# Turning a norm's column into a row: four fp32 products with the identity in place of two ones-by-diagonal products

## The chip, the cores and the metric

The kernel runs on one core of one Trainium2 chip. The metric is the device time of one execution in microseconds (us); lower is better. A core has a matrix engine (PE, with its weight loads shown as PEld), a vector engine (DVE), an activation engine (ACT), a general engine (POOL) and a queue engine (SP) that issues most loads. Each engine runs its own instructions strictly in the order in which the program placed them; an instruction that waits holds all that stand behind it on that engine.

## The reference

One decoder layer on x of 512 tokens by 1024: a SwiGLU feed-forward (FFN 1, width 2816), a mixer (a state-space group "SSD" with 16 heads in 4 groups, and differential attention with 8 heads, sharing an input and an output projection), cross-attention into a memory of 256 tokens, a second feed-forward (FFN 2), a final norm. What matters here is the norm:

```python
def rms_norm(x, w):
    x32 = x.astype(jnp.float32)
    y = x32 * lax.rsqrt(jnp.mean(x32 * x32, axis=-1, keepdims=True) + EPS)
    return y.astype(x.dtype) * w
...
    yg = y.reshape(bsz, seqlen, SSD_GROUPS, SSD_WIDTH // SSD_GROUPS)
    yg = yg * lax.rsqrt(jnp.mean(yg * yg, axis=-1, keepdims=True) + EPS)
```

It is taken over x ahead of FFN 1, the mixer, the cross-attention and FFN 2, over the memory, and over each of the four SSD groups: one number per token each time. (The heads' norm and the final norm don't use the code below.)

## The kernel before

Activations lie transposed: features on the 128 partitions, tokens along the free dimension (512 fp32 numbers, which is one accumulator bank). So one number per token is needed as a *row*: the same 512 numbers on every partition. The square sums come out of the matrix engine as a *column* (`nps` or `pn`, 128 partitions x 4 blocks of tokens); `inv_rms_cols` makes `ncol`, 1/rms, on DVE (`nv`) and POOL (`pow`). In the SSD groups `rh` is half of it.

`row_of(col, nb, first, second)` turns the column into a row in the bank `nrow`. It splits the column into a high part `ch` (rounded to fp32r, the format in which the matrix engine takes one pass) and a rest `cl`, builds for each a diagonal `ndiag` (identity times column, 128 x 512), and multiplies a matrix of ones (`ones_r`, stationary) with the two diagonals, adding both in `nrow`. The engine of the diagonals is DVE for the five `Stat` norms (FFN 1, memory, mixer, cross, FFN 2) and POOL for the four SSD groups. `Stat.finish` then copies `nrow` to `row` on ACT; the SSD group multiplies `y` with `nrow` on DVE (L935), and splits the result into `ysh` (ACT) and `ysl` (DVE).

All large products are made in three fp32r products of high and low parts. `load_w` loads a weight tile (`wr`, 6 buffers), and splits it into `wh` on ACT and `wl` on DVE (3 buffers each). Products accumulate in 8 banks, 4 named acc and 4 aux. The names of accumulators tell the stage: `pv`, `pq`, `pk` the attention's projections, `pxbc`, `pz` the SSD group's, `pm` the output projections, `pcv` the values of the cross-attention, `pst`, `pf`, `py` the SSD scan, `pcb` four 128 x 128 products of two fp32 tensors at the start of each SSD group, `qa`, `qb`, `qe` the FFN quads.

The order of the work is fixed when the program is built. `Order` runs a dense stream of projections and side chains (the SSD groups, the heads, the norms). Its clock `od.t` is advanced by `mm` with each product (one pass for fp32r, four for fp32), and a chain's `yield W[...]` says how much of that clock is to pass before its next step is written. The engines' own order of ACT and DVE comes from a list scheduler on the same program; SP and POOL stand as written.

Around the third SSD group (g = 2) the dense stream is `pz`, then `out_attn(1, 5, 8)`: three output tiles `pm` of 12 products each, for x[5], x[6], x[7], then `pcv`. The raw weights of these three tiles are loads of `in_woa`; `memory_prep` loads eight tiles `mem` there.

Of the kernel before, what the change touches and what calls it, by code (L numbers as in the profile page):

```python
# [11 lines left out]
F32 = mybir.dt.float32  # L12
R32 = mybir.dt.float32r
AF = mybir.ActivationFunctionType
ALU = mybir.AluOpType
AX = mybir.AxisListType

P = 128
# [82 lines left out]
def body(tc, a, dbg=None):  # L101
# [6 lines left out]
    tiny = ctx.enter_context(tc.tile_pool(name="tiny", bufs=6))  # L108
# [6 lines left out]
    def nm(s):  # L115
        uid[0] += 1
        return f"{s}_{uid[0]}"

    def s2(s, dt=F32, shape=(P, T)):
        if math.prod(shape[1:]) <= T // 2:  # L120
            return sp.tile(list(shape), dt, tag="s1", name=nm(s), bufs=NHALF)
        return sp.tile(list(shape), dt, tag="s2", name=nm(s))
# [4 lines left out]
    def small(s, n, bufs=None):  # L127
        return tiny.tile([P, n], F32, tag=s, name=nm(s), bufs=bufs)
# [4 lines left out]
    def aux(s, shape=(P, T)):  # L133
        return aux_p.tile(list(shape), F32, tag="aux", name=nm(s))
# [5 lines left out]
    last, start, last_sum, recent, newest, newest_mm = [], [], [], [], [], []  # L140
    V, S, G = nc.vector, nc.scalar, nc.gpsimd
    od = Order()

    def mm(out, w, x, start, stop):
        od.t += (1 if w.dtype == R32 else 4) * (x.free_size() + 8) / 2400
        newest_mm[:] = [nc.tensor.matmul(out, w, x, start=start, stop=stop).ins]  # L146
# [36 lines left out]
    @contextmanager  # L183
    def behind(ins):
        with ExitStack() as after:
            for i in ins:
                after.enter_context(tc.issue_after(i))
            yield
# [146 lines left out]
    ident = cp.tile([P, P], F32, name="ident")  # L335
# [3 lines left out]
    ones_r = cp.tile([P, P], R32, name="ones_r")  # L339
# [13 lines left out]
    def inv_rms_cols(ps, nb, scale, eps):  # L353
        v = small("nv", nb)
        V.tensor_scalar(v, ps, scale, eps, ALU.mult, ALU.add)
        col = small("ncol", nb, bufs=6)
        G.tensor_tensor(col, v, mhalf[:, :nb], ALU.pow)
        return col

    def row_of(col, nb, first, second):  # L360
        ch = tiny.tile([P, nb], R32, tag="ch", name=nm("ch"))
        V.tensor_copy(ch, col)
        cl = small("cl", nb)
        V.tensor_tensor(cl, col, ch.bitcast(F32), ALU.subtract)
        pr = aux("nrow", (P, nb * P))
        for j, (eng, c) in enumerate(((first, ch.bitcast(F32)), (second, cl))):
            diag = s2("ndiag", R32, (P, nb, P))
            eng.tensor_tensor(diag, ident[:, None, :].to_broadcast([P, nb, P]), c[:, :, None].to_broadcast([P, nb, P]), ALU.mult)  # L368
            with behind(list(newest_mm)):
                mm(pr, ones_r, diag.rearrange("p a b -> p (a b)"), j == 0, j == 1)  # L370
        return pr

    class Stat:
# [14 lines left out]
        def finish(self, apart=2.5):  # L388
            nb = self.n // P
            ps = aux("nps", (P, nb))  # L390
            for b in range(nb):
                mm(ps[:, b : b + 1], self.acc[:, b * P : (b + 1) * P], ones[:, 0:1], True, True)
            self.col = inv_rms_cols(ps, nb, 1.0 / D, EPS)
            yield apart
            pr = row_of(self.col, nb, V, V)
            self.row = s2("row", shape=(P, nb * P))
            S.activation(self.row, pr, AF.Copy)

# [408 lines left out]
    def group_dense(g):  # L807
        bc, xs, zs = [], [], []
        yield from xbc_tile(8 + g, bc)
        yield from xbc_tile(12 + g, bc)  # L810
        for j in range(2):
            yield from xbc_tile(2 * g + j, xs)
        od.spawn(group(g, bc[0], bc[1], xs, zs), W["g0"])
        for j in range(2):
            ps = acc("pz")
            yield from proj(ps, load_w(a["wz"][2 * g + j]), h)
            zs.append(silu2(ps))
# [11 lines left out]
    def group(g, bt, ct, xs, zs):  # L829
# [99 lines left out]
        rh = small("rh", 4)  # L929
        V.tensor_scalar(rh, rr, 0.5, None, ALU.mult)  # L930
        yield W["gn"]
        pr = row_of(rh, 4, G, G)
        for j in range(2):
            n = 2 * g + j
            V.scalar_tensor_tensor(yz[j], yz[j], par[:, C_SSD + n : C_SSD + n + 1], pr, ALU.mult, ALU.mult)  # L935
# [468 lines left out]
```

## Time and profile before

| what | us |
|---|---|
| median of 3 runs (1333.7, 1337.35, 1333.83) | 1333.83 |
| the profiled execution | 1333.16 |
| its span, first to last instruction | 1331.4 |
| PE busy | 1305.6 (98%) |
| DVE busy | 976.2 (73%) |
| ACT busy | 663.0 (50%) |
| POOL busy | 112.3 (8%) |

The profiled execution is 0.67 us under the median; 1.8 us of it lie outside the span. A row of the profile's timeline reads: start in the span (us), duration (us), engine, line of the code, operation, output tile and input tiles, count, and in brackets how long the engine sat idle before it and what ended that. In a row of waits, `PE pm L146 <- ACT wh L155: 5.7, 1, 5.7` says that PE's instruction writing `pm` waited for ACT's `wh`: total us, times, longest. An fp32 product shows as two instructions, so four of them as x8; ends of products are modelled, so what one costs in a busy stream is read from start to start.

### The profile page before, as it was taken

The page shows a single profiled execution, that of the slowest core. Times are in us where ns is not written, and L with a number is a line of the kernel's source. Part 1 is how long each engine was busy: PE and PEld are TensorE (multiplying, and loading weights), DVE is VectorE, ACT ScalarE, POOL GpSimd, SP SyncE. Part 2 cuts the span into 40 slices and gives each one's busy share as a digit, 9 for nine tenths or more (in the row PEclk, how much of TensorE's full clock was granted, in tenths as well). Part 3 has the DMA queues.
Part 4 walks back from the last instruction along what each step waited for, and adds up shares of the span by engine and source line. Part 5 has one row for each costly group of instructions (what it writes and reads, how often), then busy time and mean ns, then how long its engine had stood idle before and what let it go on. Part 6 is the DMA issues. An engine that isn't in the chain of part 4 may idle for free. (4 is left out here: it accounts for less than half of the span.)

```text
span 1331.4 us, 20052 instructions
## 1 busy us (share of the span) xinstructions
PE 1305.6 (98%) x7769; PEld 1136.6 (85%) x7769; DVE 976.2 (73%) x1528; ACT 663.0 (50%) x1114; POOL 112.3 (8%) x127
## 2 busy tenths in 40 slices
PE   8999999999999999999999989999999999999997
PEld 7898998899887778777788868888889999989995
DVE  6874778487885786647767776656678878887896
ACT  6442445154453564336644645434455545554564
POOL 0000010000010011200112021120001100000001
PEclk9999999999999999999999999999999999999999
DMA  7444577556464435763276477786239776666762
GB/s 271 111 127 127 127 198 246 134 145 172 128 234 151 126 87 128 225 200 99 60 208 197 109 205 225 200 208 173 61 114 244 205 224 175 190 193 174 194 200 95
DMA packets 67999, 222.71 MB, mean 167 GB/s; under 512 B 8424, under 2 KB 11984, under 8 KB 67552
## 3 DMA queue, kind: packets, MB, share of 16 engines
q1 hardware_dynamic: 52400, 174.42, 39.3%
q0 software_dynamic: 11904, 40.45, 17.1%
q10 hardware_dynamic: 3600, 6.56, 1.5%
q8 instruction: 61, 1.00, 0.3%
q14 instruction: 34, 0.28, 0.1%
HBM read 219.24 MB, written 50.91 MB: 203 GB/s over the span
## 5 line engine op out<-in xcount | busy, mean ns | idle before, releaser
L155 ACT ACTIVATE wh<-wr 128x1024 fp32r<-128x1024 f32 (+2 forms) x311 | 316.8, 1021 | 382.7 <-PE po L146 61.7
L156 DVE TENSOR_TENSOR wl<-wr,wh 128x1024 fp32r<-128x1024 f32 (+2 forms) x311 | 367.2, 1183 | 116.9 <-ACT wh L155 114.0
L146 PE MATMUL po<-gh,wh 128*128 128x512 f32 x176 | 68.8, 392 | 0.0
L146 PE MATMUL po<-gl,wh 128*128 128x512 f32 x176 | 68.5, 390 | 0.0
L146 PE MATMUL po<-gh,wl 128*128 128x512 f32 x176 | 68.4, 389 | 0.0
L240 PE MATMUL qa<-hml,wh 128*128 128x256 f32 x216 | 61.1, 283 | 0.0
L240 PE MATMUL qa<-hmh,wl 128*128 128x256 f32 x216 | 61.1, 283 | 0.0
L240 PE MATMUL qa<-hmh,wh 128*128 128x256 f32 x216 | 61.1, 283 | 0.0
L146 PE MATMUL pxbc<-hnh,wh 128*128 128x512 f32 x128 | 52.1, 407 | 0.0
L146 PE MATMUL pxbc<-hnl,wh 128*128 128x512 f32 x128 | 50.2, 392 | 0.0
L146 PE MATMUL pxbc<-hnh,wl 128*128 128x512 f32 x128 | 50.2, 392 | 0.0
L706 ACT ACTIVATE ec<-ec,mn 128x512 f32<-128x512 f32 (+3 forms) x64 | 35.5, 555 | 24.8 <-DVE mn L705 24.7
L511 DVE TENSOR_TENSOR upd<-po,row 128x512 f32<-128x512 f32 x24 | 16.6, 690 | 39.1 <-PE po L146 38.8
L240 PE MATMUL qe<-s31h,wl 128*128 128x256 f32 x152 | 43.2, 284 | 0.5 <-DVE wl L156 0.5
L240 PE MATMUL qb<-s24h,wl 128*128 128x256 f32 x152 | 43.1, 284 | 0.5 <-DVE wl L156 0.5
L240 PE MATMUL qe<-s31h,wh 128*128 128x256 f32 x152 | 43.1, 284 | 0.0
L240 PE MATMUL qe<-s24h,wh 128*128 128x256 f32 x152 | 43.0, 283 | 0.0
L240 PE MATMUL qb<-hmh,wh 128*128 128x256 f32 x152 | 43.0, 283 | 0.0
L240 PE MATMUL qb<-hml,wh 128*128 128x256 f32 x152 | 43.0, 283 | 0.0
L240 PE MATMUL qb<-hmh,wl 128*128 128x256 f32 x152 | 43.0, 283 | 0.0
L240 PE MATMUL qe<-s24h,wl 128*128 128x256 f32 x152 | 43.0, 283 | 0.0
L240 PE MATMUL qb<-s31h,wl 128*128 128x256 f32 x152 | 43.0, 283 | 0.0
(444 smaller groups left out, 4063.3 us busy)
## 6 DMA issues: line engine op xcount, KB each, us to landing
wr<-in_f2q SPq DMA_DIRECT2D x44, 512.0 KB, 4.4
wr<-in_f1q SPq DMA_DIRECT2D x40, 512.0 KB, 4.1
isum<-in_f2q SPq DMA_DIRECT2D x22, 512.0 KB, 5.7
wr<-isum SPq DMA_DIRECT2D x22, 512.0 KB, 4.4
wsum<-in_f2b SPq DMA_DIRECT2D x20, 512.0 KB, 6.2
wr<-wsum SPq DMA_DIRECT2D x20, 512.0 KB, 4.2
wr<-in_f1q POOLq DMA_DIRECT2D x16, 512.0 KB, 5.6
wr<-in_f1o SPq DMA_DIRECT2D x16, 512.0 KB, 4.0
```

The lines of the kernel that those rows point to most:

```text
L146: newest_mm[:] = [nc.tensor.matmul(out, w, x, start=start, stop=stop).ins]
L155: S.activation(hi, src, AF.Copy),
L156: V.tensor_tensor(lo, src, hi.bitcast(F32), ALU.subtract),
L240: newest_mm[:] = [nc.tensor.matmul(out, a_[:, wc], b_, start=first and f == 0 and kp == 0 and j == 0, stop=kp == n - 1 and j == 2, skip_gr ...
L511: V.tensor_tensor(upd, po, row4, ALU.mult)
L706: S.activation(ec[:, :n], ec[:, :n], AF.Exp, bias=mn, scale=-1.0, accum_out=sm[c][:, i : i + 1])
```

## The change

`row_of` no longer splits the column and builds no diagonals. For each block of 128 tokens it takes one column of `col`, read with step zero as a 128 x 128 stationary operand (the same number in all columns), and multiplies it with the identity in plain fp32. The product is the column's numbers as a row on all partitions. Four products write the four quarters of `nrow` (two for the memory's norm).

```diff
-    def row_of(col, nb, first, second):
-        ch = tiny.tile([P, nb], R32, tag="ch", name=nm("ch"))
-        V.tensor_copy(ch, col)
-        cl = small("cl", nb)
-        V.tensor_tensor(cl, col, ch.bitcast(F32), ALU.subtract)
+    def row_of(col, nb):
         pr = aux("nrow", (P, nb * P))
-        for j, (eng, c) in enumerate(((first, ch.bitcast(F32)), (second, cl))):
-            diag = s2("ndiag", R32, (P, nb, P))
-            eng.tensor_tensor(diag, ident[:, None, :].to_broadcast([P, nb, P]), c[:, :, None].to_broadcast([P, nb, P]), ALU.mult)
-            with behind(list(newest_mm)):
-                mm(pr, ones_r, diag.rearrange("p a b -> p (a b)"), j == 0, j == 1)
+        with behind(list(newest_mm)):
+            for b in range(nb):
+                mm(pr[:, b * P : (b + 1) * P], col[:, b : b + 1].to_broadcast([P, P]), ident, True, True)
         return pr
...
-            pr = row_of(self.col, nb, V, V)
+            pr = row_of(self.col, nb)
...
-        pr = row_of(rh, 4, G, G)
+        pr = row_of(rh, 4)
```

Everything below `row_of` stands six lines higher in the changed file (L929 is the old L935). Up to the first SSD group the order of the matrix engine's instructions is the same but for `nrow`. After it, the clock `od.t` stands 0.47 us further on at each row (four passes of 4 x 136 columns in place of two of 520, at its 2400 columns per us), and some side steps move against the dense stream by three products or so. Three places of the third SSD group:

On ACT, ahead of that group, where the weights of the output tiles are split (`wh` of a 512-wide `wr`; `wh_7808` and `wh_7838` before are those of x[5] and x[6]). Before:

```order
L155 ACTIVATE wh_7808<-wr_7806 128x512
L920 ACTIVATE ysq_7676<-y_7669 128x512
L799 ACTIVATE conv_7685<-pxbc_7627,par 128x512
L155 ACTIVATE wh_7838<-wr_7836 128x512
L790 ACTIVATE th_1555_7690<-conv_7685 128x512
```

And now (`wh_7776` is that of x[5]):

```order
L155 ACTIVATE wh_7776<-wr_7774 128x512
L914 ACTIVATE ysq_7638<-y_7549 128x512
L914 ACTIVATE ysq_7641<-y_7634 128x512
L793 ACTIVATE conv_7653<-pxbc_7595,par 128x512
L784 ACTIVATE th_1535_7658<-conv_7653 128x512
```

The split for x[6] has left this place.

On ACT, some rows later: from the group's normed output `ysh` through the next group's decays (`e`, `gate`) to the next weights. Before (`wh_7922` is that of x[7]):

```order
L155 ACTIVATE ysh_7857<-y_7584 128x512
L155 ACTIVATE ysh_7862<-y_7669 128x512
L890 ACTIVATE e_1604_7872<-gate_7580 64x512 x2
L892 ACTIVATE gate_7580<-gate_7580,cum 128x128 x5
L893 ACTIVATE gate_7580<-gate_7580 128x512
L892 ACTIVATE gate_7580<-gate_7580,cum 128x128 x3
L159 ACTIVATE hm_7903<-mem_7887,par 128x256
L893 ACTIVATE gate_7580<-gate_7580 128x512
L159 ACTIVATE hm_7915<-mem_7889,par 128x256
L155 ACTIVATE wh_7922<-wr_7920 128x512
```

And now (`wh_7861` is that of x[6], `wh_7884` that of x[7]):

```order
L155 ACTIVATE ysh_7808<-y_7549 128x512
L155 ACTIVATE ysh_7813<-y_7634 128x512
L884 ACTIVATE e_1576_7823<-gate_7545 64x512 x2
L886 ACTIVATE gate_7545<-gate_7545,cum 128x128 x5
L887 ACTIVATE gate_7545<-gate_7545 128x512
L886 ACTIVATE gate_7545<-gate_7545,cum 128x128 x3
L159 ACTIVATE hm_7854<-mem_7838,par 128x256
L887 ACTIVATE gate_7545<-gate_7545 128x512
L155 ACTIVATE wh_7861<-wr_7859 128x512
L159 ACTIVATE hm_7874<-mem_7840,par 128x256
L155 ACTIVATE wh_7884<-wr_7882 128x512
```

Two weight splits now stand behind the decays where one stood, and one `hm` fewer is ahead of the first. On SP the load of x[6]'s weights likewise stands behind the eight `mem` loads now, and stood ahead of them.

On PE at the same place: the row, between the scan's `pst` and the output tiles (`pm_7835` and `pm_7858` are x[6]). Before:

```order
L146 MATMUL pst_7828<-xde_7765,btk_7797 128x256
L146 MATMUL pm_7835<-yah_6302,wh_7838 128x512
L146 MATMUL pm_7835<-yal_6303,wh_7838 128x512
L146 MATMUL pm_7835<-yah_6302,wl_7839 128x512
L146 MATMUL nrow_7849<-ndiag_7850,ones_r 128x512
L146 MATMUL nrow_7849<-ndiag_7853,ones_r 128x512
L146 MATMUL pst_7866<-xde_7788,btk_7797 128x256
L146 MATMUL pm_7835<-yah_6480,wh_7838 128x512
```

And now:

```order
L146 MATMUL pm_7773<-yah_6850,wl_7777 128x512
L146 MATMUL pst_7797<-xde_7744,btk_7765 128x256
L146 MATMUL nrow_7802<-ident,rh_7735 128x128 x4
L146 MATMUL pst_7817<-xde_7756,btk_7765 128x256
L146 MATMUL pm_7858<-yah_6267,wh_7861 128x512
```

The row stands three products earlier, and with it all of x[6]'s 12 products stand behind the row.

## The prediction

> **What bounds the kernel.** I read the page's busy times first, then PE's table of waits.
>
> ```profile
> PE 1305.6 (98%) x7769; PEld 1136.6 (85%) x7769; DVE 976.2 (73%) x1528; ACT 663.0 (50%) x1114; POOL 112.3 (8%) x127
> ```
>
> PE is busy 98% of the span, so a microsecond of PE work is a microsecond of the end, and work taken off DVE or POOL counts only where PE waits for it. Where does it wait?
>
> ```profile
> PE pm L146 <- ACT wh L155: 5.7, 1, 5.7
> ...
> PE pv L146 <- DVE kl L156: 2.2, 1, 2.2
> PE pt L150 <- DVE on L766: 1.3, 1, 1.3
> ```
>
> Three waits matter, each once. The first two lie beside a `nrow`, so the sum has three parts: PE's own work for the nine rows, the wait of `pv`, and the wait of `pm`.
>
> **PE's work for the rows.** Before, a row is two products; read from its start to the start of the next instruction.
>
> ```profile
> 367.13 1.10 PE L146 MATMUL nrow<-ndiag,ones_r 128*128 128x512 f32 x2 [0.33 <-DVE ndiag L368]
> 368.07 0.40 PE L146 MATMUL pck<-hm,wh 128*128 128x256 f32 x2
> ...
> 569.31 0.62 PE L146 MATMUL nrow<-ndiag,ones_r 128*128 128x512 f32 x2
> 569.77 0.40 PE L146 MATMUL pv<-wh,hnh 128*128 128x512 f32 x1
> ...
> 878.53 1.01 PE L146 MATMUL nrow<-ndiag,ones_r 128*128 128x512 f32 x2
> 879.37 0.39 PE L146 MATMUL pcq<-hmh,wh 128*128 128x512 f32 x1
> ...
> 1004.08 0.40 PE L146 MATMUL nrow<-ndiag,ones_r 128*128 128x512 f32 x1
> 1005.02 0.50 PE L146 MATMUL nrow<-ndiag,ones_r 128*128 128x512 f32 x1 [0.55 <-DVE ndiag L368]
> 1005.36 0.27 PE L240 MATMUL qb<-s31h,wh 128*128 128x256 f32 x1
> ```
>
> Undisturbed a row costs 0.46 (569.31 to 569.77). I take that for the four SSD groups and, as an estimate, for FFN 1's row. The memory's, half as wide, is taken as 0.23; the mixer's costs 0.33 + 0.94 = 1.27, the cross-attention's 0.84, FFN 2's 1.28: the last three wait for the second diagonal, which DVE makes more slowly than PE uses it. Sum: 5 x 0.46 + 0.23 + 1.27 + 0.84 + 1.28 = 5.9 us.
>
> After, a row is four fp32 products of 128 columns. The same thing stands in the trace: `pcb` is four of them, with four stationary tiles, into one bank.
>
> ```profile
> 516.31 1.05 PE L146 MATMUL pcb<-th,th 128*128 128x128 f32 x8
> 517.20 0.60 PE L150 MATMUL pxt<-ident,th 128*128 128x128 f32 x4
> 517.55 0.48 PE L146 MATMUL pz<-hnh,wh 128*128 128x512 f32 x1
> 517.87 0.40 PE L146 MATMUL pz<-hnl,wh 128*128 128x512 f32 x1
> ```
>
> It takes 0.89 us. The first wide product behind a run of short ones takes 0.32 (517.55 to 517.87), 0.09 over the 0.23 of its kind in the rows at 788 below. So 8 x 0.98 for the full rows and 0.45 + 0.09 for the memory's: 8.4 us. The column is ready before its old diagonals were, and the row's place in PE's stream isn't earlier than that, so I count no wait. **This part: +8.4 - 5.9 = +2.5 us.** That leaves open what a stationary operand read with step zero costs; nothing in the trace loads one. The low end is `pcb`'s own price, nothing added. The high end is that each of the 68 loads (34 products, two each) stands bare once more, at
>
> ```profile
> L146 PEld LDWEIGHTS pcb<-th,th x32: 187/192/192, 516.1 to 777.2; 128*128 128x128 f32 x32
> ```
>
> 68 x 0.192 = 13.1 us. I take the low end: `pcb` is the same load but for the step.
>
> **The removed DVE and POOL work.** DVE loses 18 small operations and ten diagonals. Its cover is PE's stream: apart from the waits counted above, no PE wait hangs on them, so they count for nothing. POOL loses its eight diagonals, and one pair of them is on the path, though nothing waits for it. DVE's timeline:
>
> ```profile
> 561.86 3.45 DVE L156 TENSOR_TENSOR wl<-wr,wh 128x1024 fp32r<-128x1024 f32 x1
> 565.23 0.68 DVE L156 TENSOR_TENSOR kl<-pk,kh 128x512 fp32r<-128x512 f32 x1
> ```
>
> POOL at that time:
>
> ```profile
> 561.89 1.32 POOL L368 TENSOR_TENSOR ndiag<-ident,ch 128x512 fp32r<-128x512 f32 x1
> 562.90 1.31 POOL L368 TENSOR_TENSOR ndiag<-ident,cl 128x512 fp32r<-128x512 f32 x1
> ```
>
> And all splits of that size, grouped (busy us, mean ns of one):
>
> ```profile
> L156 DVE TENSOR_TENSOR wl<-wr,wh 128x1024 fp32r<-128x1024 f32 x280 | 344.0, 1230 | 111.3 <-ACT wh L155 109.2 <-DMA isum<-in_f2q 0.5 <-DMA wr<-in_wcq 0.2
> ```
>
> And PE in that stretch:
>
> ```profile
> 563.39 0.39 PE L146 MATMUL pv<-wh,hnh 128*128 128x512 f32 x1
> 565.96 0.50 PE L146 MATMUL pv<-wh,hnh 128*128 128x512 f32 x1 [2.18 <-DVE kl L156]
> ```
>
> This `wl` takes 3.45 us where the mean of 280 is 1.23. The 2.2 us too many are the stretch from 561.9 to 564.2 in which POOL makes its diagonals: DVE's operation on two SBUF inputs stands still meanwhile. `kl` is queued behind it, and PE waits for `kl` because that frees the bank of the fourth `pv`. Without the diagonals `wl` ends near 563.0 and `kl` near 563.7, when PE needs it (563.62). Of the 2.57 us between the two `pv`, 0.23 is work; I also count the 0.1 by which PE's first product after a wait is longer. **This part: -2.4 us.** Ends: 0 if something else holds `kl`, -2.4.
>
> **The wait of `pm`, third SSD group.** PE's timeline:
>
> ```profile
> 788.43 0.39 PE L146 MATMUL pm<-yal,wh 128*128 128x512 f32 x1
> 788.66 0.39 PE L146 MATMUL pm<-yah,wl 128*128 128x512 f32 x1
> 794.71 0.79 PE L146 MATMUL pm<-yah,wh 128*128 128x512 f32 x1 [5.67 <-ACT wh L155]
> ```
>
> DVE just before:
>
> ```profile
> 786.10 0.42 DVE L871 TENSOR_TENSOR st<-st,cdec 128x256 f32<-128x256 f32 x1
> 786.59 1.41 DVE L935 SCALAR_TENSOR_TENSOR y<-y,par,nrow 128x512 f32<-128x512 f32 x2
> ```
>
> And ACT, the start and the end of its block:
>
> ```profile
> 787.37 1.29 ACT L155 ACTIVATE ysh<-y 128x512 fp32r<-128x512 f32 x2 [2.70 <-DVE y L935]
> ...
> 793.65 0.49 ACT L159 ACTIVATE hm<-mem,par 128x256 fp32r<-128x256 f32 x1
> 794.05 0.61 ACT L155 ACTIVATE wh<-wr 128x512 fp32r<-128x512 f32 x1
> ```
>
> PE has finished x[6] and waits for x[7]'s weights, which ACT splits only behind `ysh` and the decays, without a pause from 787.37 on. In the new order the weights of x[6] stand there too. So PE gets no further than the third `pst`, and waits with 24 products to do instead of 12: 12 x 0.227 = 2.7 us more work behind the wait. What does it get back? The row stands 0.9 us earlier on PE, but DVE's `y` has `st` at 786.10 to 786.52 ahead of it either way, so ACT's block starts only some 0.13 earlier; and one `hm` fewer (793.65 to 794.05, 0.40) precedes the split. **This part: +2.7 - 0.5 = +2.2 us**; the wait itself grows from 5.7 to about 8. Ends: 0 if the place of x[6]'s split doesn't matter, +2.7 if ACT starts no earlier.
>
> Behind the wait the clock matters. The busy time of the engines in one stretch, with the granted clock third from the end:
>
> ```profile
> 794.70:800.90 6.20, 6.19 (x15) 4.71 (x16) 4.97 (x9) 4.11 (x6) 0.00 (x0) 0.50 0.69 232
> ```
>
> For 6.2 us PE's granted clock is 0.50, which costs 3.1 us. By this row the longer wait costs the same, and the sum is unchanged. The Trainium skill (TensorE: Matmul & The Clock Gate, section "What's actually happening") has a free-running window of about 3.4 us: half speed after an idle window, full speed after a busy one. By that, an estimate, the slow stretch lasts 3.4 to 6.8 us and costs 1.7 to 3.4, so the sum would lie between 1.4 us lower and 0.3 higher, differing from one execution to the next. The trace agrees that a stall of 5.7 us is followed by half speed; how the stretch varies no run here shows.
>
> **Moved steps elsewhere.** Between 590 and 640 us the heads' steps slide by about three products against `pq` and `pk`, which changes PE's cover there. Some waits may shrink and others grow; a new one is priced by the 1.3 us of `pt`, either way. I take 0.
>
> **The sum.** +2.5 - 2.4 + 2.2 = +2.3 us on the profiled execution's 1333.16: 1335.5. The median of the runs lies 0.67 above that execution, which is the noise of a run; I keep 1335.5, that is 0.1% over the median. What a measurement here can tell from no change is 0.3%, 4.0 us: faster is under 1329.8, slower over 1337.8.
>
> **Rivals.**
> 1. *The long wait goes.* If x[6]'s and x[7]'s weights come before PE needs them, 5.7 + 3.1 us vanish: 1333.2 + 2.5 - 2.4 - 8.8 = 1324.5. For it: the row is ready earlier. Against it: ACT's order is fixed, and `ysh` and the decays, 6.7 us from 787.37 to 794.05, stand ahead of the split. Chance 0.05, and 0.03 for smaller gains beyond the bound.
> 2. *The step-zero load is slow.* It ends on the slower side: 1333.2 + 2.3 + up to 13.1 = 1348.6. It decides from 2.3 us, that is 0.034 us for each of the 68 loads. Against it: the load is of one number a partition instead of 128. Chance 0.08.
> 3. *New waits among the heads or behind the long one.* Two of 1.3 us on top of the sum: 1338.1. For it: the steps do move, and DMA and ACT run only some microseconds ahead. Chance 0.12, three quarters of it beyond the bound.
> 4. *The wait of `pm` stays as it was*: 1333.16 + 0.1 = 1333.3. Chance 0.14.
> 5. *The wait of `pv` stays*, because the loads that feed DVE are late and not POOL's diagonals: 1335.5 + 2.4 = 1337.9, about on the bound. Chance 0.08.
>
> My forecast, between 1333.5 and 1337.5, has the remaining 0.50.
>
> **Range and chances.** From 1331.0 (the forecast with the shortest slow stretch, or the case where `pm`'s wait doesn't grow and one wait of 1.3 us goes) to 1339.5 (two new waits and a slow median); left out are rival 1, rival 2 and a little of the third. Faster 0.08. Slower: 0.08 of rival 2, 0.09 of rival 3 and 0.02 of rival 5, 0.19. Same: 0.73.
>
> **What would show it.** Nine `nrow` groups of x8 (x4 for the memory) at 0.89 from start to next start, with no `ndiag` among PE's waits; a `wl` of 1.2 us near 562 and no wait of `pv` for `kl`; a wait of `pm` for `wh` of about 8 us near 786, with both x[6] and x[7] behind it and a granted clock of 0.5 after it. Rows well over 0.89 would be rival 2; a `pm` wait of 6 us or none would prove the third part wrong; new rows in PE's table of waits are rival 3.

## The result and the profile after

| kernel | median us | lowest to highest | runs | ratio to before, 95% |
|---|---|---|---|---|
| before, beside it | 1333.98 | 1332.95 to 1337.35 | 14 | |
| changed | 1331.93 | 1330.42 to 1333.81 | 14 | 0.9981 [0.9973, 0.9988] |

The change makes the kernel 0.19% faster, 2.5 us by the ratio, with an interval from 1.6 to 3.6. That is inside the 0.3% at which "same" ends, and inside the range of the prediction; but the forecast was +2.3 us, and the sign is the opposite. The profiled execution of the changed kernel took 1332.84 us, 0.9 over its median, where that of before lies 0.8 under its own (1333.16 beside 1333.98). So the two traces differ by 0.3 us only, and the accounts below go by places and not by the two spans.

The page's busy times after:

```profile
PE 1307.9 (98%) x7819; PEld 1141.0 (86%) x7819; DVE 966.2 (73%) x1500; ACT 663.3 (50%) x1114; POOL 103.3 (8%) x119
```

PE is busy 2.3 us longer, DVE 10.0 shorter, POOL 9.0 shorter. And the waits of PE, as in the table of before:

```profile
PE pm L146 <- ACT wh L155: 7.4, 1, 7.4
...
PE qb L240 <- ACT u L299: 1.4, 1, 1.4
PE qe L240 <- DVE nlam L556: 0.8, 1, 0.8
```

The wait of `pv` for `kl` (2.2) is gone, as forecast; the wait of `pm` has grown from 5.7 to 7.4. But the wait of `pt` for `on` among the heads (1.3) is gone too, which was not forecast, and a new one of `qb` for ACT's `u` stands in FFN 2. The wait of `qe` for `nlam`, 0.75 us at 202.94, is in this trace alone of the twelve kept; e4 and e5, which have the same program up to there, don't have it. So I take it for this execution's and not for the change's; it is as large as most of the 0.9 us above the median.

The rows themselves, on PE's timeline:

```profile
366.67 1.05 PE L146 MATMUL nrow<-ident,ncol 128*128 128x128 f32 x8
367.48 0.48 PE L146 MATMUL pck<-hm,wh 128*128 128x256 f32 x2
...
566.51 1.05 PE L146 MATMUL nrow<-ident,rh 128*128 128x128 f32 x8
567.32 0.48 PE L146 MATMUL pv<-wh,hnh 128*128 128x512 f32 x1
567.63 0.39 PE L146 MATMUL pv<-wl,hnh 128*128 128x512 f32 x1
...
1002.45 1.05 PE L146 MATMUL nrow<-ident,ncol 128*128 128x128 f32 x8
1003.25 0.36 PE L240 MATMUL qb<-s31h,wh 128*128 128x256 f32 x1
```

A row takes 0.81 us from its start to the next start (566.51 to 567.32), no row waits for its column, and the first product behind it takes 0.31 (567.32 to 567.63), where 0.23 is its kind's usual time. The loads with step zero for the five `Stat` norms, grouped (ns, min/median/max):

```profile
L146 PEld LDWEIGHTS nrow<-ident,ncol x36: 188/190/192, 29.0 to 1003.1; 128*128 128x128 f32 x36
```

They last as long as `pcb`'s (187/192/192), and a row of them costs no more than `pcb` does (0.81 here, 0.90 in the third group below, against 0.89).

DVE near 562 us, where `wl` took 3.45 us before:

```profile
561.28 1.23 DVE L156 TENSOR_TENSOR wl<-wr,wh 128x1024 fp32r<-128x1024 f32 x1 [0.25 <-ACT wh L155]
562.42 0.68 DVE L156 TENSOR_TENSOR kl<-pk,kh 128x512 fp32r<-128x512 f32 x1
```

PE and ACT in the third SSD group:

```profile
781.53 1.05 PE L146 MATMUL nrow<-ident,rh 128*128 128x128 f32 x8
782.43 0.60 PE L146 MATMUL pst<-xde,btk 128*128 128x256 f32 x2
790.47 0.79 PE L146 MATMUL pm<-yah,wh 128*128 128x512 f32 x1 [7.44 <-ACT wh L155]
...
783.53 1.29 ACT L155 ACTIVATE ysh<-y 128x512 fp32r<-128x512 f32 x2 [2.54 <-DVE y L929]
...
789.80 0.61 ACT L155 ACTIVATE wh<-wr 128x512 fp32r<-128x512 f32 x1
```

PE stops right behind the group's last `pst`, all 24 products of x[6] and x[7] still to do, and ACT's block from `ysh` on runs without a pause up to the split.

### The profile page after: what moved, and what is told of

It reads as the page before. It is cut to its first block, busy times and chain, and to the rows that moved or that the text cites. A ratio compares the mean times of both kernels' runs of the same rounds, so it can differ in the third digit from the quotient of the medians.

```text
span 1331.1 us, 20098 instructions
## 1 busy us (share of the span) xinstructions
PE 1307.9 (98%) x7819; PEld 1141.0 (86%) x7819; DVE 966.2 (73%) x1500; ACT 663.3 (50%) x1114; POOL 103.3 (8%) x119
## 5 line engine op out<-in xcount | busy, mean ns | idle before, releaser
L240 PE MATMUL qb<-s31h,wh 128*128 128x256 f32 x152 | 43.2, 284 | 1.4 <-ACT u L299 1.4
L240 PE MATMUL qb<-s24h,wh 128*128 128x256 f32 x152 | 43.0, 283 | 0.0
```

Source lines behind the costliest of these rows:

```text
L240: newest_mm[:] = [nc.tensor.matmul(out, a_[:, wc], b_, start=first and f == 0 and kp == 0 and j == 0, stop=kp == n - 1 and j == 2, skip_gr ...
```

## The experiments

Two parts of the change can be taken apart: the *work* (four products, no diagonals) and the *order* (the planner's clock stands 0.47 us further on at each row). The theory after the first comparison was ORDER: the heads' waits went because the steps slid there. The rivals were WORK (DVE and POOL have less to do) and CHANCE. Times are given with the ratio to the kernel before, run on the same chip; a ratio of 0.9990 is 1.3 us.

**e1_old_order.** The clock is set back behind each row:

```diff
     def row_of(col, nb):
         pr = aux("nrow", (P, nb * P))
+        t = od.t + 2 * (nb * P + 8) / 2400
         with behind(list(newest_mm)):
             for b in range(nb):
                 mm(pr[:, b * P : (b + 1) * P], ...)
+        od.t = t
         return pr
```

> The four fp32 products, but the planner's clock is advanced at each row as it was before, so the rest of the work stands in the old order. Theory ORDER (the heads' two waits, 0.47 and 1.32 us, went because the steps there slid against the dense stream; the long wait of pm grew for the same reason): both heads' waits are back, the wait of pm for wh is about 5.7 us with 12 products behind it, the wait of pv for kl is gone; sum from the kernel before: rows +0.9, pv -2.3, heads 0, pm 0, so -1.4 us (1332.6 beside 1334.0). Theory WORK (the heads' waits went because PE reaches them at another moment of DVE's and ACT's work, or because DVE has less to do): both waits stay away, the wait of pm is 5.7; rows +0.9, pv -2.3, heads -2.4: -3.8 us (1330.2). Theory CHANCE (the heads' waits come and go from one execution to the next): no rule, and e1's and e2's profiles need not differ there.

**e2_new_order.** The kernel before, its clock advanced as in the changed one, at the end of the old `row_of`:

```diff
+        od.t += nb * 4 * (P + 8) / 2400 - 2 * (nb * P + 8) / 2400
         return pr
```

> The old two products with their diagonals, but the planner's clock is advanced at each row as in the changed kernel, so the rest stands in the new order. Theory ORDER: the heads' two waits are gone (-2.4), the wait of pm is 7.4 to 8 us with 24 products behind it (+2.2), pv waits for kl as before with POOL's diagonals beside a wl of some 3.4 us: together -0.2 us (1333.8 beside 1334.0). Theory WORK: the heads' waits are there, so +2.2 us (1336.2). Theory CHANCE: as for the run before.

Measured: e1 1331.17 us, 0.9982 [0.9973, 0.9990]; e2 1332.95 us, 0.9999 [0.9990, 1.0008]. PE's waits of e1, and then of e2:

```profile
PE pm L146 <- ACT wh L155: 5.7, 1, 5.7
...
PE pt L150 <- DVE on L762: 1.3, 1, 1.3
...
PE ps L146 <- DVE kl L156: 0.5, 1, 0.5
```

```profile
PE pm L146 <- ACT wh L155: 7.4, 1, 7.4
...
PE pv L146 <- DVE kl L156: 2.2, 1, 2.2
```

This is what ORDER expected, wait by wait: the heads' two waits and the 5.7 us of `pm` belong to the old order, whatever the rows are made of; the wait of `pv` belongs to the diagonals. WORK falls. So does CHANCE: the heads' two waits stand in all three traces in which the heads have the old order (before, e1, e3) and in none of the nine others. The times fit less well. e2's -0.1 us [-1.3, +1.1] is ORDER's -0.2, with WORK's +2.2 outside; but e1's -2.4 [-3.6, -1.3] lies between ORDER's -1.4 and WORK's -3.8, so there the waits decide and not the time. How the `pt` wait comes and goes is seen on PE and DVE, e1 first, then e2:

```profile
632.86 0.28 PE L146 MATMUL ps<-kh,ql 64*128 64x128 f32 x2
634.46 0.41 PE L150 MATMUL pt<-ident,ec 128*128 128x128 f32 x2 [1.33 <-DVE on L762]
...
633.63 0.69 DVE L762 TENSOR_TENSOR on<-ptk,rr 128x512 f32<-128x512 f32 x1 [0.93 <-POOL rr L760]
```

```profile
634.90 0.28 PE L146 MATMUL ps<-kh,ql 64*128 64x128 f32 x2
635.11 0.44 PE L150 MATMUL pt<-ident,ec 128*128 128x128 f32 x2
...
635.27 0.69 DVE L767 TENSOR_TENSOR on<-ptk,rr 128x512 f32<-128x512 f32 x1 [1.15 <-POOL rr L765]
```

In the old order `pt` starts when `on` is done, and `on` waits for POOL's `rr`. In the new one `pt` runs before `on` does, although `on` waits longer there (1.15). That `pt` wants the bank which `on` reads is how I understand it; the rows show the dependence, not the bank.

**e3_dve_diag.** The kernel before with the SSD groups' diagonals on DVE, which takes these diagonals from POOL, gives them to DVE, and changes nothing else:

```diff
-        pr = row_of(rh, 4, G, G)
+        pr = row_of(rh, 4, V, V)
```

> The kernel before, with the diagonals of the SSD groups made by DVE instead of POOL. Theory POOL (POOL's two diagonals hold DVE's wl near 562 us, and kl and PE's pv with it): no wl there above 1.3 us on account of POOL, no wait of pv for kl, -2.3 us; against it four rows that wait for DVE's second diagonal, at the price of the mixer's and the cross-attention's rows (0.84 to 1.27 instead of 0.46): +1.5 to +3.2. Sum -0.8 to +0.9 us. Rival LATE LOADS (the weights are late and wl is long for that): wl stays near 3.4 us and pv waits 2.2 us; +1.5 to +3.2 us. Rival QUEUE (DVE itself is full there): pv waits, behind the two diagonals on DVE (1.4 us) instead of beside POOL's.

Measured: 1330.73 us, 0.9975 [0.9965, 0.9986]. DVE near 562 us:

```profile
561.13 1.23 DVE L156 TENSOR_TENSOR wl<-wr,wh 128x1024 fp32r<-128x1024 f32 x1
562.27 0.68 DVE L156 TENSOR_TENSOR kl<-pk,kh 128x512 fp32r<-128x512 f32 x1
562.87 0.68 DVE L368 TENSOR_TENSOR ndiag<-ident,ch 128x512 fp32r<-128x512 f32 x1
563.47 0.69 DVE L368 TENSOR_TENSOR ndiag<-ident,cl 128x512 fp32r<-128x512 f32 x1
```

POOL's diagonals held `wl`, shown: without them it takes 1.23 us at the same place, and `pv` no longer waits. The expected price of diagonals on DVE (+1.5 to +3.2) did not come: on this timeline they are ready at 564.2, PE reaches the row at 566.32, and none of the four rows waits. So this edit of one line is measured at 0.25% where the whole change has 0.19%; the two intervals overlap, so that it is the larger gain is not shown.

**e9_heads_order_only.** The clock is advanced in the new way at the first four rows only, in the old way from the second SSD group on:

```diff
+        t = od.t + 2 * (nb * P + 8) / 2400
...
+        rows_made.append(pr)
+        if len(rows_made) > 4:
+            od.t = t
```

> The changed kernel, but the planner's clock is advanced by four fp32 products only at the first four rows (FFN 1, memory, mixer, first SSD group), and as before at the later ones. So the heads stand in the new order and the third SSD group in the old one. Theory ORDER IN TWO PLACES: no waits of pt and ps among the heads (-2.4 us against the run in the old order), the wait of pm is 5.7 us with 12 products behind it (-2.2 against the changed kernel): 1328.8 to 1329.7. Rival ONE MOVES THE OTHER (PE arriving at the third group 2.4 us earlier only waits longer there, because ACT's block is timed by DVE and the loads): the wait of pm grows to about 8 and the time is 1331 to 1332.

Measured: 1328.83 us, 0.9967 [0.9955, 0.9980]. PE's waits:

```profile
PE pm L146 <- ACT wh L155: 5.7, 1, 5.7
PE init L342 <- ACT ones_r L340: 2.4, 1, 2.4
PE qb L240 <- ACT u L299: 0.5, 1, 0.5
PE pq L146 <- ACT wh L155: 0.4, 1, 0.4
```

Both effects of the order stand by themselves, and this kernel has the good half of each. Against e1, PE's starts move by 2.3 us between 622 and 640 us; built with the clock advanced at the first three rows alone, the program has the order of e1 on every engine, so it is the first SSD group's row that makes the heads' gain. Against the changed kernel the third group saves 1.8 us of the wait, and 0.0014 of the ratio is 1.9 us. PE arriving there earlier did not lengthen the wait: ACT's block comes earlier with it.

**e7_dve_diag_new_order.** The kernel before with the edits of e2 and e3 together: old products, no diagonals on POOL, new order.

```diff
+        od.t += nb * 4 * (P + 8) / 2400 - 2 * (nb * P + 8) / 2400
...
-        pr = row_of(rh, 4, G, G)
+        pr = row_of(rh, 4, V, V)
```

> The old products with the new order, as in the second run, and the SSD groups' diagonals on DVE. What is left between it and the changed kernel is the row itself (two products with diagonals on DVE, against four products) at one order, without POOL's diagonals in both. If the terms add: the second run's no change, and -2.5 to -3 us for POOL's diagonals: 1330.4 to 1331 (-1 us against the changed kernel, if its rows cost 0.9 us more and the wait of u 1.4, less 0.7 of waits for wl near 270 us). Theory PRODUCTS HELP: the changed kernel is at least as fast as this one. The waits of pv and of the heads are absent, the wait of pm is 7.4.

Measured: 1329.66 us, 0.9971 [0.9962, 0.9981]. Beside the changed kernel's 0.9981 it suggests that the four products are no gain in themselves: at the same order, with POOL free of diagonals in both, the kernel with the old two-product rows is measured 1.3 us faster. The intervals overlap, so the sign is likely and not shown.

**e8_rows_twice.** Each row's products twice into the same bank, the clock advanced once:

```diff
-            for b in range(nb):
+            t = od.t + nb * 4 * (P + 8) / 2400
+            for b in [*range(nb), *range(nb)]:
...
+            od.t = t
```

> The changed kernel with each row's products written twice into the same bank: 34 fp32 products more, nothing else moved on PE. Price of a full row by the trace after 0.80 to 0.81 us from start to next start, of the memory's 0.36: if that is what they cost, +6.8 us (1338.7, ratio to the kernel before 1.0033). By the prediction's 0.98 a row: +8.3 (1340.2). If the load with step zero is partly hidden by the row's position and costs more in a longer run, above that. Rival SLACK: some rows stand right before waits (pm), which swallow one: +6.

Measured: 1338.17 us, 1.0032 [1.0020, 1.0044], that is 6.8 us over the changed kernel's ratio.

```profile
568.38 1.95 PE L146 MATMUL nrow<-ident,rh 128*128 128x128 f32 x16
570.09 0.48 PE L146 MATMUL pv<-wh,hnh 128*128 128x512 f32 x1
```

Eight products take 1.71 from start to next start: four followed by more fp32 products take 0.90 (as `pcb` does, 0.89, and as the row of the third group, which `pst` follows), the last four, followed by an fp32r product, 0.81, and that product then takes 0.31 in place of 0.23. So a row costs 0.89 whichever way it is read. The time agrees with the +6.8 that was expected from 0.81 a row, but in part by luck: eight more rows at 0.90 and the memory's at 0.45 are 7.65 us, and the wait of `qb` for `u`, which e8's trace doesn't have, takes about 1.0 off; the interval, some 2 us either way, excludes neither sum. The step-zero load is not slow even in a run of sixteen (187 to 192 ns): rival 2 falls.

**e5_ffn2_old_row.** The changed kernel with FFN 2's row alone in the old form (diagonals on DVE; `row_by_diagonals` is the old `row_of` with the clock advanced in the new way), order unchanged:

```diff
-            od.spawn(st_2.finish(8.0), 5.0)
+            od.spawn(st_2.finish(8.0, row_by_diagonals), 5.0)
```

> The changed kernel with FFN 2's row alone made as before (two diagonals on DVE, two products), in the same order otherwise. The profiles of the three kernels with the four products so far have a wait of qb for ACT's u near 1025 us (1.45, 1.10, 0.86), the three with diagonals have none. Theory ROW (the quicker row sends loads into each other there, and what it gains comes back as that wait): the row costs 1.28 again instead of 0.81 (+0.47) and the wait of 0.9 to 1.5 us is gone: -0.4 to -1.0 us against the changed kernel (1331.0 to 1331.5). Theory PLACE (the wait hangs on when the upstream work arrives there, not on this row): the wait stays, +0.5 us (1332.4).

Measured: 1331.45 us, 0.9985 [0.9976, 0.9993], not to be told from the changed kernel. The wait of `qb` for `u` is 0.33 instead of 1.45. Over all kernels it is 1.45, 1.10, 0.86, 1.48 and 0.51 where that row takes 0.81 us; with the row in the old form it is 0.33 here and absent there in before and in e2, e3, e7 and e10 (e7 has 0.24 of its kind later, at 1041.58), and it is absent in e8, whose row takes 1.70. So it goes with the quick row, and takes back what the row gains there. On ACT `u` stands behind weight splits for which ACT had waited for a load of `in_f2q`, 4.91 us in the changed kernel and 3.80 here; why a quicker row makes that load late was not followed.

**e4_early_weights.** The long wait of `pm` is older than the change, and the runs point at it. In the changed kernel the weights of x[6] and x[7] are loaded and split together with x[5]'s:

```diff
+        ws = {}
         for o in range(o0, o1):
             po = acc("pm")
-            yield from proj(po, load_w(a["woa"][hg, o], 4 * P), heads)
+            for n in range(o, min(o + (2 if prep else 0), o1 - 1) + 1):
+                if n not in ws:
+                    ws[n] = load_w(a["woa"][hg, n], 4 * P)
+            yield from proj(po, ws.pop(o), heads)
```

> The changed kernel, but where the output tiles of the third SSD group begin, the weights of x[6] and x[7] are loaded and split together with x[5]'s, so that none of the three splits stands behind ysh and the decays on ACT. If the long wait of pm comes from the place of that split alone: the wait of 7.4 us and the half-speed stretch behind it (3.1 us) vanish, -10.5 us (1321.4 beside 1331.9 of the changed kernel, ratio to the kernel before about 0.9905). If the half clock is the price of that wait, none below 1.0 is seen from 780 to 810 us. Rival: three pairs of split weights fill their three buffers each, and the splits for the next products (pcv) come late: a new wait of 2 to 6 us near 795 us, and a gain of only 3 to 8 us.

Measured: 1327.06 us, 0.9947 [0.9933, 0.9961]. The rival was right: all three splits stand ahead of `ysh`, `pm` doesn't wait, and `pcv` waits behind the same block on ACT instead. So the gain is 4.5 us over the changed kernel's ratio and not 10.5; half clock still follows the wait, for 3.4 us.

```profile
790.76 0.73 PE L146 MATMUL pcv<-wh,hm 128*128 128x512 f32 x2 [3.21 <-ACT wh L155]
...
789.66 1.04 ACT L155 ACTIVATE wh<-wr 128x1024 fp32r<-128x1024 f32 x1
```

**e6_cover_more.** So the block needs more PE work behind the row, split before it. On top of e4, five output tiles stand behind the groups instead of three, `memory_prep` starts earlier, and `pcv`'s first weights are loaded where x[6] begins:

```diff
-SPLIT, AHEAD = 5, 2
+SPLIT, AHEAD = 3, 2
...
-            od.spawn(memory_prep(hm2, 1.5), 4.0)
+            od.spawn(memory_prep(hm2, 2.0), 0.5)
...
+            if prep and o == 6:
+                wcv0.append(load_w(a["wcv"][0]))
...
-            w = load_w(a["wcv"][k])
+            w = wcv0.pop() if wcv0 else load_w(a["wcv"][k])
```

> The early weights, with more of the dense stream behind the third group's row: out_attn of the second half is cut at tile 3 instead of 5, so five output tiles stand behind the groups, their weights split two tiles ahead; the memory tiles are prepared earlier, and pcv's first weights are loaded with x[6]'s. In the run with early weights pcv waited 3.2 and 0.5 us behind the decays, and 3.4 us of half clock followed (1.7 us lost). Theory COVER (ACT's block of about 7 us behind the row only has to be covered by PE work whose weights are split): 48 products, 10.9 us, cover it; the wait of pcv is 0 to 1.5 us, no half clock: -3 to -5.4 us against the run with early weights (1321.7 to 1324). Rival TAKEN FROM ELSEWHERE: the two tiles moved away leave the second group (730 to 770 us) without cover, a new wait of 1 to 3 us there: 1323 to 1327.

Measured: 1322.91 us, 0.9921 [0.9909, 0.9933]. In one stretch, the engines' busy time, then clock, DMA share and GB/s:

```profile
776.00:800.00 24.00, 24.00 (x139) 20.05 (x138) 21.75 (x36) 19.41 (x41) 0.00 (x0) 1.00 0.81 227
```

PE is busy throughout at full clock. The rival is there as well, but small: `pn` waits 1.26 us for POOL's squares at 717 us. This is the fastest of all kernels here, 10.5 us under the kernel before, and 8 us of that are the old wait of `pm` and not the change.

**e10_dve_diag_cover.** e6 with the two-product rows, all diagonals on DVE: the old `row_of` with e2's line, and

```diff
-            pr = row_of(self.col, nb)
+            pr = row_of(self.col, nb, V, V)
...
-        pr = row_of(rh, 4)
+        pr = row_of(rh, 4, V, V)
```

> The kernel with more cover behind the third group's row, but its rows made by the old two products, all diagonals on DVE, and the planner's clock as in the changed kernel. If the terms add (this row form was about 1.3 us faster than four products, by ratios 0.9971 against 0.9981): 1321.6 beside 1322.9, ratio to the kernel before about 0.991. Rival: DVE is busier in the shortened second group (the wait of pn for the squares near 717 us, 1.26 us, gets longer), and nothing is gained: 1323 to 1325.

Measured: 1323.24 us, 0.9924 [0.9912, 0.9937]: no gain over e6. In its profile the 1.26 us of `pn` were followed by 3.4 us of half clock, 1.7 us lost, which e6's profile doesn't have; whether the row form is worth anything here stays open.

## Why the prediction was right or wrong

**The step that failed: "Moved steps elsewhere ... I take 0."** The heads' slide is worth -2.2 us: the waits of 0.47 and 1.32 go, and with them the slower start behind each. Instruction by instruction, PE's starts move by 2.3 us between e1 and e9 and by 2.2 between before and e2, at 622 to 640 us both times. The text had named the place, the three products of slide and the 1.3 us of `pt`, and priced the wait correctly; it then took the middle of "either way". But the table of before had two waits standing there that a slide could remove, and no row for one that it could add, so the middle was not zero.

**The wait of `pv`: right.** -2.4 forecast; laid beside before, instruction by instruction, PE's starts move by 2.3 us in e1 and in the changed kernel and by 2.2 in e3 at that place, and e3 shows that it was POOL's two diagonals.

**The wait of `pm`: right in mechanism, 0.4 too large.** x[6]'s split standing behind `ysh` and the decays lengthens the wait from 5.67 to 7.44 with 24 products behind it, in the changed kernel and (7.40) in e2, not in e1 and e9. Forecast "about 8" and +2.2; the wait grows by 1.77, and the ratios of e9 and the changed kernel differ by 1.9 us. What was too large is the "+2.7". The group's row stands between x[5]'s last product and the stop, and it takes 0.90 now (781.53 to 782.43 above) where it took 0.47:

```profile
785.92 0.62 PE L146 MATMUL nrow<-ndiag,ones_r 128*128 128x512 f32 x2
786.39 0.59 PE L146 MATMUL pst<-xde,btk 128*128 128x256 f32 x2
```

So from the start of x[5]'s last product PE gets to the stop in 2.16 us (780.87 to 783.03) in place of 4.48 (784.56 to 789.04): 2.32 less, not 2.7. The row's own 0.43 us, counted in the first part, is taken off this wait. The two amounts set against it were right: ACT's block starts 0.15 earlier by the same measure (forecast 0.13), and is 0.41 shorter by the one `hm` (0.40). The row stands 0.70 earlier and not 0.9, which changes nothing here.

That the slow stretch costs the same after either wait held only roughly:

```profile
788.40:795.22 6.82, 4.75 (x11) 3.67 (x12) 5.62 (x10) 5.08 (x11) 0.00 (x0) 0.50 0.37 105
```

It is 6.8 us long again, but begins 2.1 us before PE resumes, so that 4.75 us of work ran in it: 2.4 us lost instead of 3.1. Over the nine traces that have this wait the loss (half of what PE works in the stretch) is 2.4 to 3.1 us behind 5.7 us (before, e1, e3, e9) and 1.5 to 2.8 behind 7.3 or 7.4 (the changed kernel, e2, e5, e7, e8). It varies by a microsecond from one execution to the next, and with one trace a kernel I put no difference into the sum.

**"This part: +8.4 - 5.9 = +2.5 us": mis-sized.** The new rows cost 8 x 0.89 + 0.45 = 7.6, where the text had 8 x 0.98 + 0.54: it added 0.09 for the slower first product behind a row to `pcb`'s 0.89, which already holds it (0.81 + 0.08). The old ones were dearer by FFN 1's, taken as 0.46:

```profile
29.87 0.75 PE L146 MATMUL nrow<-ndiag,ones_r 128*128 128x512 f32 x2
30.46 0.39 PE L146 MATMUL pg<-hmh,wh 128*128 128x512 f32 x1
```

It takes 0.59, so 6.0 in all. The term is +1.6.

**"No PE wait hangs on them, so they count for nothing": wrong by 0.7.** Before, the memory norm's four DVE operations stand just ahead of a `wl` that PE waits for at 267.83; four us later there is another such wait.

```profile
265.88 0.42 DVE L368 TENSOR_TENSOR ndiag<-ident,ch 128x256 fp32r<-128x256 f32 x1
266.22 0.42 DVE L368 TENSOR_TENSOR ndiag<-ident,cl 128x256 fp32r<-128x256 f32 x1
266.55 1.22 DVE L156 TENSOR_TENSOR wl<-wr,wh 128x1024 fp32r<-128x1024 f32 x1
...
267.83 0.39 PE L240 MATMUL qe<-s31h,wl 128*128 128x256 f32 x1 [0.48 <-DVE wl L156]
...
271.50 0.38 PE L240 MATMUL qb<-s24h,wl 128*128 128x256 f32 x1 [0.53 <-DVE wl L156]
```

In the changed kernel and in e1 only 0.33 of the two is left; in e2, e3 and e7, which keep those diagonals, both stand as they were.

**A new wait that no part had.** `qb` for `u`, 0.5 to 1.5 us in the five kernels with the quick FFN 2 row.

Put together: +1.6 - 2.3 - 2.2 + 1.8 - 0.7 + 1.0 = -0.8 us, against +2.3 forecast and -2.5 [-3.6, -1.6] measured. Of the error of 4.8 us the terms explain 3.1: heads 2.2, rows 0.9, DVE 0.7, `pm` 0.4, less the new wait's 1.0, and 0.1 of `pv` the other way. What is left is 1.7. It is not the order, since e2, which has the order alone, gives -0.1 where its terms say -0.4. Kernels without POOL's diagonals are all faster than their terms, e3 too (-3.3 measured, -2.2 on the trace). One thing that would do part of it was seen in one trace, that of e2: half clock behind the wait of `pv`.

```profile
562.50:565.90 3.40, 1.22 (x6) 0.71 (x5) 2.91 (x2) 0.00 (x0) 3.40 (x5) 1.00 0.99 152
565.96:569.37 3.41, 3.41 (x10) 2.63 (x9) 0.00 (x0) 0.00 (x0) 0.22 (x1) 0.50 1.10 320
```

It costs 1.7 us more where it happens, and the trace of before, which has the same wait, doesn't show it. The mean granted clock that is on record for each run tells how often it may happen: a stretch of 3.4 us at half clock lowers the mean over 1331 us by 0.0013. Of the 53 runs of the kernel before that were made beside the experiments, 23 have a mean clock of 0.994, with a median of 1334.3 us, and 30 have 0.995 or 0.996, with 1332.7. Of the 24 runs of e1, e3 and e9, which have no wait of `pv` and the same 5.7 us of `pm`, none has 0.994. So I take it, as an estimate, for four executions in ten, 0.7 us on average; where in those runs the clock fell no trace shows. About 1.0 us of the remainder stays open.

Of the rivals, the third was nearest to what happened, with the sign turned: waits among the heads went instead of coming. The first ("the long wait goes") would have needed the splits ahead of `ysh`; e4 and e6 do that by hand and gain 4.5 and 8 us over the changed kernel. That 1331.93 lies inside the stated range speaks for nothing: its low end, 1331.0, does not follow from the two cases named for it, which give 1335.5 - 1.4 = 1334.1 and 1335.5 - 2.2 - 1.3 = 1332.0.

## What to carry to other kernels

Where a program's order is set by a clock, an edit that changes the price of one step moves everything behind it, and the move can be worth as much as the edit: here -2.2 and +1.8 us beside +1.6 and -2.3. Build the edit with the old order and the old code with the new order before giving the edit the credit, and follow each known wait through both orders instead of taking zero. And a wait of 6 to 7 us that an edit only shifts is worth more than the edit: give the engine that waits enough work whose inputs are prepared ahead of the block.

## What the runs showed of the hardware

- DVE and POOL: a DVE operation on two SBUF inputs (128x1024) took 3.45 us while POOL ran two 128x512 products of two SBUF inputs, and 1.23 at the same place without them. The 2.2 us are nearly the whole time of POOL's two operations (561.89 to 564.21, 2.3 us): DVE stood, it was not slowed. A tiny DVE operation beside POOL shows the same: `cl`, which takes 0.16 us elsewhere, took 1.00 and ended with POOL's operation, at 782.9.

```profile
781.92 1.00 DVE L364 TENSOR_TENSOR cl<-rh,ch 128x4 f32<-128x4 f32 x1
...
781.77 1.13 POOL L368 TENSOR_TENSOR ndiag<-ident,ch 128x512 fp32r<-128x512 f32 x1 [1.02 <-PE pz L146]
```

The Trainium skill (GPSIMD Engine Reference, section "8. Key points") says that POOL shares its SBUF interfaces with DVE, with contention where DVE has two SBUF inputs; the runs agree, and give the size.
- A stationary operand read with step zero costs what any other 128x128 fp32 one does: 187 to 192 ns a load, hidden as well as `pcb`'s.
- The clock falls in whole steps. Half-speed stretches lasted 3.4 us (e2, e4, e10), 6.8 (before, after, e1, e3, e5, e7, e9) and 10.2 (e2 and e8, behind `pm`), whatever the wait before them, 1.26 to 7.4 us. The Trainium skill (TensorE: Matmul & The Clock Gate, section "What's actually happening") has a free-running window of 3413 ns, and these are one, two and three of it. By that page the clock falls after an idle window; the rows differ there, since in e2 PE was busy 1.22 of the 3.40 us ahead of the stretch. In e10 it was busy even for 2.15 of 3.42:

```profile
717.10:720.52 3.42, 2.15 (x14) 1.61 (x13) 1.87 (x4) 0.49 (x1) 2.79 (x3) 1.00 0.55 109
720.52:723.93 3.41, 3.41 (x9) 2.64 (x8) 2.41 (x7) 1.30 (x2) 2.37 (x3) 0.50 0.96 184
```

So a wait of 1.3 us cost 3.0 in e10's trace, with the half clock behind it, and 1.3 in e6's.
